# One chunk of three feed-forward stages: seven block products of sums of blocks in place of eight

## The chip, the cores and the metric

The kernel runs on one core of one Trainium2 chip. The metric is the device time of one execution in microseconds. A core has a TensorE (PE; its weight loads are listed apart as PEld), a VectorE (DVE), a ScalarE (ACT), a GpSimd (POOL) and a SyncE (SP), whose queue issues nearly all transfers here. Each engine takes its instructions in order; semaphores tie them together.

## The reference

Two layers of a decoder trunk, for 256 tokens of width 1024, in float32. Each layer is a feed-forward half step, a token mixer, and a second feed-forward half step, each with a norm before and after:

```python
def swiglu(x, w_gate, w_up, w_down):
    return (jax.nn.silu(x @ w_gate) * (x @ w_up)) @ w_down

    for layer in range(DEPTH):
        ng = norm_gains[layer]
        hdn = swiglu(rmsnorm(x, ng[0]), ffn1_w_gate[layer], ffn1_w_up[layer], ffn1_w_down[layer])
        x = x + 0.5 * rmsnorm(hdn, ng[1])
        hdn = rmsnorm(x, ng[2])
        ...
        x = x + rmsnorm(hdn, ng[3])
        hdn = swiglu(rmsnorm(x, ng[4]), ffn2_w_gate[layer], ffn2_w_up[layer], ffn2_w_down[layer])
        x = x + 0.5 * rmsnorm(hdn, ng[5])
```

`w_gate` and `w_up` are 1024 x 2816, `w_down` is 2816 x 1024. The mixers (sparse attention with a state-space branch in layer 0, RWKV-7 in layer 1) are not touched by the change.

## The kernel before

The stages run one after another: f10 (first feed-forward half step of layer 0), the mixer of layer 0, f20, then f11, the mixer of layer 1, f21. The 256 tokens are two tiles of 128, t = 0 and t = 1; the normed input x lies transposed in two tiles, `xth` and `xtl`.

**Numbers.** A float32 product is made of three matmuls: each operand is split into a high and a low part (`hi` rounded, `lo` the rest), and high x high, high x low and low x high are added up in a PSUM bank `acc` (`mm3`). For the weights this split is work on every load: a raw unit of 512 KB lands in `raw`, ScalarE writes `whi` (with the norm's gain `gch`, where there is one), and VectorE writes `wlo` from `raw` and `whi` (`unit`). Both go into a ring of ten pairs of buffers (`rings`: six of the pool ringb, four of ringa). A pair is given back when both token tiles have been multiplied by it.

**A feed-forward stage** (`ffn`) has 66 units in a row: 5 chunks of 512 gate and 512 up columns with 8 units each (one unit is 128 rows k of both), 4 units for the last 256 columns, and 22 units of `w_down`. `lagged` goes through them: unit i is split and multiplied for t = 0, and for t = 1 some units later (`lag`, LAG units at most). After the last row of a chunk, `chunk_end` applies silu and the product with up into `sg`, PE transposes it, and `hth` and `htl` (high and low part) are kept for `w_down`. At the start of a stage, `entry` puts the second token tile's transposes and splits (`prenorm`) between the first units.

**Order.** The program is written in this order; a scheduler in the framework then orders the instructions of each engine inside a stage by its own estimates. Transfers stand in SP's queue in the order of `loads`; one whose buffer is not free holds up those behind it. All instructions of PE, VectorE and ScalarE are issued in `_Engine`'s `call`, so that in the profile of before they stand at L112 (the transfers of the raw units at L288); in the changed file these lines are L130 and L307.

Of the kernel before, what the change touches and what calls it, by code (L numbers as in the profile page):

```python
# [11 lines left out]
F32 = mybir.dt.float32  # L12
F32R = mybir.dt.float32r
# [15 lines left out]
Q_COLS = [(64 * (4 * v + g), 64 * (4 * v + g) + 64) for g in range(4) for v in range(2)]  # L29


def _ffn_units(which, layer):
    units = []
    for c in range(5):
        for k in range(KD):
            units.append((((f"{which}_w_gate", layer), (f"{which}_w_up", layer)), k, 1, [(512 * c, 512 * c + 512)]))
    for h in range(4):
# [22 lines left out]
def _weight_units():  # L60
    a, b, c, o = _mix0_units()
    cg = lambda n: [((n, 0), 4 * h, 4, [(256 * c, 256 * c + 256)]) for c in range(4) for h in range(2)]
    sq = lambda n: [((n, 0), k, 1, [(0, D)]) for k in range(KD)]
    return {
        "f10": _ffn_units("ffn1", 0),
        "m0a": a, "m0x": b, "m0z": c, "m0o": o,
        "f20": _ffn_units("ffn2", 0),
        "f11": _ffn_units("ffn1", 1),
        "m1l": [((("c_w1", 0), ("c_a1", 0)), 0, 8, [(0, 64)])],
        "m1k": cg("c_w_k"),  # L70
        "m1r": cg("c_w_r"),
        "m1g": [(("c_g1", 0), 4 * h, 4, [(0, 160)]) for h in range(2)],
        "m1v": [(("c_w_v", 0), 2 * h, 2, [(512 * c, 512 * c + 512)]) for c in range(2) for h in range(4)],
        "m1o": sq("c_w_o"),
        "f21": _ffn_units("ffn2", 1),
    }


# [19 lines left out]
    return kt, n * sum(hi - lo for lo, hi in cols)  # L98


class _Engine:

    def __init__(self, trunk, engine, kind):
        self.trunk, self.engine, self.kind, self.last = trunk, engine, kind, None

    def __getattr__(self, name):
        f = getattr(self.engine, name)

        def call(out, *a, **k):
            r = f(out, *a, **k)  # L112
            if self.trunk.strict:
# [3 lines left out]
                self.last = r.ins.name  # L117
# [136 lines left out]
class _Trunk:  # L254
# [268 lines left out]
    def lagged(self, units, work, at={}, lag=lambda i: LAG, start=0):  # L523

        pend = []
        for i, u in enumerate(units):
            if i < start:
                continue
            if i in at:
                at[i]()  # L530
            while len(pend) > lag(i - 1):
                work(1, *pend.pop(0))
            w = self.ahead.pop(0) if self.ahead else self.unit(u, self.gain(units, i))
            work(0, i, w)
# [12 lines left out]
    def ffn(self, units, gpost, last, kind, ahead=(), after=None, first=False):  # L547

        nc, tc = self.nc, self.tc
        st = {}  # L550
        hth = {}
        htl = {}

        def chunk_end(t, c, gate, up, n):
            sg = self.wk.tile([P, 512], F32, name="sg", tag="sg", bufs=2)
            r = self.r[t]
            nc.scalar.activation(sg[:, :n], gate, AF.Silu, scale=r)
            nc.vector.scalar_tensor_tensor(sg[:, :n], up, r, sg[:, :n], op0=ALU.mult, op1=ALU.mult)
            if c not in hth:
                hth[c] = hp.tile([P, n // P, S], F32R, name="hth", tag=f"hth{c}")  # L560
                htl[c] = hp.tile([P, n // P, S], F32R, name="htl", tag=f"htl{c}")
# [6 lines left out]
            nc.vector.tensor_sub(htl[c][:, :nj, ts], tp[:, :nj, :], hth[c][:, :nj, ts].bitcast(F32))  # L568

        def work(t, i, w, hs=(0, 1), between=None):  # L570
            wh, wl = w
            ts = slice(P * t, P * t + P)
            xh, xl = [a[:, :, ts] for a in self.xt]
            if i < 40:
                c, k = i // 8, i % 8
# [16 lines left out]
            elif i < 44:  # L592
                c, h = 5, i - 40
                if h == 0:
                    st[t] = self.acc.tile([P, 512], F32, name="acc", tag="acc")
                a = st[t]
                for k in range(2):
                    kk = 2 * h + k
                    self.mm3(a, xh[:, kk, :], xl[:, kk, :], wh[:, k, :], wl[:, k, :], kk == 0, kk == 7)
                if h == 3:  # L600
                    chunk_end(t, c, a[:, :256], a[:, 256:], 256)
            else:
                ft = i - 44
                if ft == 0:
                    for h in hs:
                        st[t, "y", h] = self.acc.tile([P, 512], F32, name="acc", tag="acc")
                for h in hs:
                    self.mm3(st[t, "y", h], hth[ft // 4][:, ft % 4, ts], htl[ft // 4][:, ft % 4, ts],
                             wh[:, 0, 512 * h:512 * h + 512], wl[:, 0, 512 * h:512 * h + 512],
                             ft == 0, ft == 21)  # L610

        n = len(units)
        with tc.tile_pool(name="hp", bufs=1, reuse_waits="tile") as hp, self.work_pool():
            if first:
                self.begin(units, work)
# [1878 lines left out]
    def run(self):  # L2494
# [8 lines left out]
        with self.raw_pool(), ExitStack() as ring:  # L2503
            ring.enter_context(self.ring())
            self.ffn(ph["f10"], 1, 2, "mixer", ph["m0a"], first=True)
            self.mix0(ph, 3, 2, ring, self.y1)
            self.ffn(ph["f20"], 5, 6, "ffn", ph["f11"])
            a, b = [self.ringa], self.rings[:1]
            self.rings = a * 4 + (b * 6 + a * 2) * 2 + (b * 6 + a * 4) * 4 + b * 6
            self.count = len(self.ahead)  # L2510
            self.ffn(ph["f11"], 7, 8, "plain", after=lambda: self.mix1_start(ph["m1l"][0]))
        y = self.mix1(ph, 9, self.y1)
        with self.raw_pool(side="right"), self.ring():
            with self.work_pool():
                row = self.row(9, tag="raw", bufs=None, pool=self.raw)
                self.prepare(ph["f21"], 1)
                self.postnorm(1, y, row, False)
            self.ffn(ph["f21"], 11, None, "out")
        banks.close()


# [85 lines left out]
```

## Time and profile before

| | before |
|---|---|
| median of 3 runs | 1171.52 us (1171.45 to 1172.55) |
| profiled execution | 1170.79 us |
| its span | 1169.0 us, mean granted clock 0.999 |
| PE busy | 1153.5 us, 6855 matmuls |
| VectorE busy | 778.9 us |
| ScalarE busy | 598.1 us |
| moved | 192.43 MB, 165 GB/s on average |

The span goes from the first to the last instruction in the profile; the time of an execution holds a little more around it. Busy times are those of the profiled execution. PE is listed as busy for nearly the whole span; how near it is to its own limit is read from the spacing of its matmuls and from what it waits for. The page's sums are means over six unlike stages; the change touches three of them, f20 (about 383 to 569 us in the span), f11 (569 to 756) and f21 (980 to 1165).

### The profile page before, as it was taken

How to read it: one execution, taken by the hardware profiler on the slowest of the kernel's cores; microseconds unless marked ns; L12 is line 12 of the kernel's file. 1: busy time of each engine (PE TensorE's matmuls, PEld its weight loads, DVE VectorE, ACT ScalarE, POOL GpSimd, SP SyncE). 2: the span in 40 equal slices, each digit the busy share in tenths (PEclk: the TensorE clock that was granted, in tenths of full speed). 3: DMA queues.
4: the chain of work that ended last, by engine and by line, in shares of the span. 5: the costliest groups of instructions: out<-in, count | busy, mean ns of one | idle time of the engine just before them, and what ended most of it. 6: DMA issues, size and time to landing. Idle time of an engine off the chain costs nothing.

```text
span 1169.0 us, 17703 instructions
## 1 busy us (share of the span) xinstructions
PE 1153.5 (99%) x6855; PEld 975.2 (83%) x6855; DVE 778.9 (67%) x1310; ACT 598.1 (51%) x1000; POOL 17.3 (1%) x46
## 2 busy tenths in 40 slices
PE   9999999999999999999999999999999999999997
PEld 7888888898998788888888888899988887888886
DVE  6675547888779855554856555578885797655543
ACT  6655445677575655543555544375054145645431
POOL 0000000000000000000000000002100000000000
PEclk9999999999999999999999999999999999999999
DMA  8866564443335765555456555711334123765540
GB/s 288 282 209 187 180 201 145 148 136 102 108 128 166 241 207 186 189 181 184 149 190 225 189 180 198 261 37 57 112 110 146 36 95 121 241 207 185 180 162 37
DMA packets 54163, 192.43 MB, mean 165 GB/s; under 512 B 6653, under 2 KB 6653, under 8 KB 53950
## 3 DMA queue, kind: packets, MB, share of 16 engines
q1 hardware_dynamic: 54078, 191.30, 49.9%
q8 instruction: 54, 0.88, 0.3%
q14 instruction: 31, 0.25, 0.1%
HBM read 190.22 MB, written 1.05 MB: 164 GB/s over the span
## 4 chain that ended last, share of the span: by engine, by line
PE 92%; DVE 4%; DMA 1%; ACT 1%; issue 1%; SPq 0%; DVEq 0%; ACTq 0%; POOL 0%; POOLq 0%
PE acc L112 87%; PE tp L112 5%; DMA raw<-in_wst_dram 1%; DVE wlo L112 1%; ACT whi L112 1%; ACT junk L112 0%; DVE rs_a L112 0%; DVE xu L112 0%; DVE tm L112 0%; DVE lc L112 0%; DVE x L112 0%; DVE rs_y L112 0%; SPq L288 0%; DVE wl L112 0%; ACT aT L112 0%
## 5 line engine op out<-in xcount | busy, mean ns | idle before, releaser
L112 DVE SCALAR_TENSOR_TENSOR wlo<-raw,gch,whi 128x1024 fp32r<-128x1024 f32 (+2 forms) x211 | 236.3, 1133 | 125.8 <-ACT whi L112 125.4
L112 ACT ACTIVATE whi<-raw,gch 128x1024 fp32r<-128x1024 f32 (+2 forms) x211 | 213.2, 1029 | 151.3 <-PE acc L112 99.4
L112 PE MATMUL acc<-whi,xth 128*128 128x512 f32 (+1 forms) x576 | 224.4, 393 | 0.8 <-ACT whi L112 0.6
L112 PE MATMUL acc<-wlo,xth 128*128 128x512 f32 (+1 forms) x576 | 223.2, 389 | 0.2 <-DVE wlo L112 0.2
L112 PE MATMUL acc<-whi,xtl 128*128 128x512 f32 (+1 forms) x576 | 222.8, 388 | 0.0
L112 DVE TENSOR_TENSOR wlo<-raw,whi 128x1024 fp32r<-128x1024 f32 x112 | 137.1, 1224 | 116.2 <-ACT whi L112 115.9
L112 ACT CAST whi<-raw 128x1024 fp32r<-128x1024 f32 x112 | 117.7, 1051 | 124.7 <-PE acc L112 110.4
L112 PE MATMUL acc<-whi,hth 128*128 128x512 f32 x352 | 137.5, 391 | 0.0
L112 PE MATMUL acc<-whi,htl 128*128 128x512 f32 x352 | 137.0, 389 | 0.0
L112 PE MATMUL acc<-wlo,hth 128*128 128x512 f32 x352 | 137.0, 389 | 0.0
L112 PEld LDWEIGHTS acc<-whi,xth 128*128 128x128 f32 x576 | 108.1, 188 | 23.0 <-ACT whi L112 1.5
L112 PEld LDWEIGHTS acc<-whi,xtl 128*128 128x128 f32 x576 | 108.1, 188 | 21.9 <-DVE xtl L112 0.4
L112 PEld LDWEIGHTS acc<-wlo,xth 128*128 128x128 f32 x576 | 108.2, 188 | 21.2 <-DVE wlo L112 0.6
L112 PE MATMUL acc<-whi,xt 128*128 128x512 f32 x352 | 111.0, 391 | 0.0
L112 PEld LDWEIGHTS acc<-whi,htl 128*128 128x128 f32 x352 | 66.1, 188 | 13.8
L112 PEld LDWEIGHTS acc<-whi,hth 128*128 128x128 f32 x352 | 66.1, 188 | 13.6
L112 PEld LDWEIGHTS acc<-wlo,hth 128*128 128x128 f32 x352 | 66.1, 188 | 13.5
L112 PEld LDWEIGHTS acc<-whi,xt 128*128 128x128 f32 x352 | 66.0, 188 | 13.5
L112 PE MATMUL acc<-wlo,xt 128*128 128x512 f32 x176 | 69.0, 392 | 0.0
L112 PE MATMUL acc<-xnh,whi 128*128 128x256 f32 x160 | 46.6, 291 | 0.0
L112 PE MATMUL acc<-xnl,whi 128*128 128x256 f32 x160 | 45.2, 282 | 0.0
L112 PE MATMUL acc<-xnh,wlo 128*128 128x256 f32 x160 | 45.2, 282 | 0.0
(369 smaller groups left out, 1673.7 us busy)
## 6 DMA issues: line engine op xcount, KB each, us to landing
raw<-in_wst_dram SPq DMA_DIRECT2D x300, 512.0 KB, 3.6
lw<-in_wst_dram SPq DMA_DIRECT2D x12, 512.0 KB, 3.5
grow<-in_rows_dram SPq DMA_DIRECT2D x8, 512.0 KB, 4.8
wlo<-in_wst_dram SPq DMA_DIRECT2D x8, 512.0 KB, 3.7
whi<-in_wst_dram SPq DMA_DIRECT2D x8, 512.0 KB, 4.2
wr<-in_wst_dram SPq DMA_DIRECT2D x8, 512.0 KB, 5.7
rows<-in_rows_dram SPq DMA_DIRECT2D x3, 512.0 KB, 5.4
lw<-in_lw_dram SPq DMA_DIRECT2D x3, 512.0 KB, 3.6
```

Source lines behind the costliest of these rows:

```text
L112: r = f(out, *a, **k)
```

## The change

In f20, f11 and f21 (not in f10), chunk 3 (`WIDE`) of the gate and up columns is computed as a product of 2 x 2 blocks: rows are the two token tiles, the inner dimension is halved (4 of the 8 rows k each), columns are gate and up. The eight block products of the plain way become seven, of sums and differences of blocks.

- *Loads.* Chunk 3's eight units become four of 1 MB, issued after the units k = 4 to 7 of chunk 2. Two land in a new buffer `wa`, two in a buffer `hx`, and ScalarE scales them in place with the gain.
- *Sums of x* (`sums`, at unit 10): VectorE adds `xth` and `xtl` to x again, forms four sums of blocks, and splits them with ScalarE into `sumh` and `suml`. `pin` ties the first of these instructions to stand behind VectorE's last instruction written so far.
- *Products* (`spread(None)`, before chunk 4): seven phases of two ring units with six matmuls each, 84 matmuls where there were 96. Before a phase VectorE forms, where needed, the difference or sum of two weight blocks in place; then ScalarE casts and VectorE subtracts, as for any weight. Three partial results are copied by ScalarE to `u` tiles, and VectorE adds a bank to each.
- *Both token tiles* take part in every phase, so the lag of t = 1 goes down towards chunk 3 and up again behind it. `rings`' order changes with it.
- `hth` and `htl` of chunks 3 to 5 are kept in `hx`, which is first the room for the sums, then for raw weights. In f20 and f21 the row of gains for the norm behind the stage is fetched into an `xp` tile before the last four loads, and a small VectorE copy goes away.

```diff
+WIDE = 3
-def _ffn_units(which, layer):
+def _ffn_units(which, layer, wide=False):
     for c in range(5):
+        if wide and c == WIDE:
+            continue
         for k in range(KD):
             units.append((..., k, 1, [(512 * c, 512 * c + 512)]))
+            if wide and c == WIDE - 1 and k > 3:
+                j = k - 4
+                units.append((..., 2 * j, 2, [(512 * WIDE, 512 * WIDE + 512)]))
...
     def lagged(self, units, work, at={}, lag=lambda i: LAG, start=0, wide=None):
+            if _ffn_part(u)[0] == "w":
+                wide(u)
+                continue
+            if wide and _ffn_part(u) == ("g", WIDE + 1, 0):
+                while pend:
+                    work(1, *pend.pop(0))
+                wide(None)
...
+        def spread(unit):
+            if unit is not None:
...
+                if j % 2 == 0:
+                    raws[j] = wa[:, j // 2]
+                else:
+                    if j == 1:
+                        st["raw"] = space(F32)
+                    raws[j] = st["raw"][:, j // 2, 0:8]...
+                self.loads.append(self.fetch(raws[j], src, after=self.loads[-1]))
+                for i in range(2):
+                    nc.scalar.activation(raws[j][:, i], raws[j][:, i], AF.Copy, scale=g[:, i])
+                return
...
+            def phase(bank, a, b, start, before=lambda p: None):
+                for p in range(2):
+                    before(p)
+                    ring = self.rings[self.count % len(self.rings)]
+                    self.count += 1
+                    hi, lo = [ring.tile([P, 2, 512], F32R, name=g, tag=g) for g in ("whi", "wlo")]
+                    x = b(p)
+                    nc.scalar.copy(hi, x)
+                    nc.vector.tensor_sub(lo, x, hi.bitcast(F32))
+                    for j in range(2):
+                        k = 2 * p + j
+                        nc.tensor.matmul(bank, a[0][:, k], hi[:, j], ...)
+                        nc.tensor.matmul(bank, a[0][:, k], lo[:, j], ...)
+                        nc.tensor.matmul(bank, a[1][:, k], hi[:, j], ...)
+            q, r, z = acc(), acc(), acc()
+            phase(q, half(row0, 0), lambda p: g0[p], True)
+            m1 = temp()
+            nc.scalar.copy(m1, q)
+            phase(r, form(0), lambda p: t1, True, lambda p: sub(t1, u0[p], g0[p]))
+            m5 = temp()
+            nc.scalar.copy(m5, r)
+            def inner(p):
+                sub(u0[p], u1[p], u0[p])
+                nc.vector.tensor_add(g0[p], u0[p], g0[p])
+            phase(q, form(1), lambda p: g0[p], False, inner)
+            u2 = temp()
+            nc.scalar.copy(u2, q)
+            phase(r, form(3), lambda p: u1[p], False)
+            nc.vector.tensor_add(u2, u2, r)
+            phase(q, form(2), lambda p: u0[p], False)
+            nc.vector.tensor_add(m5, m5, q)
+            phase(z, half(row0, 1), lambda p: g1[p], True)
+            nc.vector.tensor_add(m1, m1, z)
+            phase(q, half(row1, 1), lambda p: g1[p], False, lambda p: sub(g1[p], g1[p], g0[p]))
+            chunk_end(0, WIDE, m1, u2, 512, m1)
+            chunk_end(1, WIDE, q, m5, 512)
+
+        def sums():
+            hi, lo = [self.xp.tile([P, 4, 4, P], F32R, name=n, tag="x8") for n in ("sumh", "suml")]
+            w = space(F32)
...
+            nc.vector.pin = True
+            for h in range(2):
+                a = [v[:, 4 * h:4 * h + 4].bitcast(F32) for v in self.xt]
+                nc.vector.tensor_add(x[:, 4 * h:4 * h + 4], *a)
+            nc.vector.tensor_add(f[:, 0], a21, a22)
+            nc.vector.tensor_sub(f[:, 1], f[:, 0], a11)
+            nc.vector.tensor_sub(f[:, 2], a11, a21)
+            nc.vector.tensor_sub(f[:, 3], a12, f[:, 1])
+            for h in range(2):
+                nc.scalar.copy(hi[:, hs], f[:, hs])
+                nc.vector.tensor_sub(lo[:, hs], f[:, hs], hi[:, hs].bitcast(F32))
...
+        def lag(i):
+            return min(LAG - 2 * (i == LAG - 1) - (LAG <= i < n - 8), max(0, (24 - i) // 2) if i < 28 else max(1, (i - 30) // 4))
...
+            space = lambda dt: hp.tile([P, 2, 10, S], dt, name="hx", tag="hx")
+            if wide:
+                wa = hp.tile([P, 2, 2, D], F32, name="wa")
...
-                rows = [self.row(gpost, after=hth[1].bitcast(F32)[:, 0, 0:1]), None]
+                row = self.xp.tile([P, 2, D], F32, name="rows", tag="x8")[:, 0]
+                self.fetch(row, self.rows[gpost].partition_broadcast(P), self.loads[-4])
+                rows = [row, None]
```

The instructions of f10 and of both mixers stand in the same order as before; what moves lies in the three stages. The first place is VectorE at the start of f20, behind the splits of the second token tile (`xtl`); the rows `rs_...` belong to the norm's square root. Before:

```order
L112 TENSOR_TENSOR xtl<-tp,xth 128x4x128
L112 TENSOR_SCALAR rs_h<-rs_h 128x1
L112 SCALAR_TENSOR_TENSOR rs_y<-rs_a,rs_y 128x1
L112 TENSOR_SCALAR rs_y<-rs_h 128x1
L112 SCALAR_TENSOR_TENSOR wlo<-raw,gch,whi 128x1024
```

And after the change:

```order
L130 TENSOR_TENSOR xtl<-tp,xth 128x4x128
L130 TENSOR_SCALAR rs_h<-rs_h 128x1
L130 SCALAR_TENSOR_TENSOR rs_y<-rs_a,rs_y 128x1
L130 TENSOR_TENSOR hx<-xth,xtl 128x1024
L130 TENSOR_SCALAR rs_y<-rs_h 128x1
L130 SCALAR_TENSOR_TENSOR wlo<-raw,gch,whi 128x1024 x2
```

The first addition of the sums stands now ahead of the split of the stage's sixth unit.

The second place is VectorE around chunk 3 of f20. Before, it holds gained splits of the weights, with `sg` and `htl` of the chunks between:

```order
L112 SCALAR_TENSOR_TENSOR wlo<-raw,gch,whi 128x1024
L112 SCALAR_TENSOR_TENSOR sg<-acc,rs_y,sg 128x512
L112 SCALAR_TENSOR_TENSOR wlo<-raw,gch,whi 128x1024 x2
L112 TENSOR_TENSOR htl<-tp,hth 128x4x128
L112 SCALAR_TENSOR_TENSOR wlo<-raw,gch,whi 128x1024 x2
```

After, the same stretch (`wa` and `hx` as a source of `wlo` are weights of chunk 3 or combinations of them):

```order
L130 TENSOR_TENSOR htl<-tp,hth 128x4x128
L130 TENSOR_TENSOR wlo<-wa,whi 128x1024
L130 SCALAR_TENSOR_TENSOR sg<-acc,rs_y,sg 128x512
L130 TENSOR_TENSOR wa<-wa 128x2x512
L130 TENSOR_TENSOR wlo<-hx,whi 128x1024 x2
L130 TENSOR_TENSOR hx<-hx 128x2x512 x2
L130 TENSOR_TENSOR htl<-tp,hth 128x4x128
L130 TENSOR_TENSOR hx<-hx 128x2x512
L130 TENSOR_TENSOR wlo<-hx,whi 128x1024
L130 TENSOR_TENSOR wlo<-wa,whi 128x1024
```

Combinations and plain splits have taken the place of the gained splits, and there are more of them in a row.

The third place is PE in chunk 3 of f20 after the change (acc_4443 and acc_4444 are the banks q and r of `spread`; acc_4629, acc_4630 and acc_4649 belong to chunk 4):

```order
L130 MATMUL acc_4444<-whi_4528,suml_4082 128x512
L130 MATMUL acc_4629<-whi_4625,xth_3821 128x512
L130 MATMUL acc_4630<-whi_4625,xth_3821 128x512
L130 MATMUL acc_4649<-whi_4625,xth_3821 128x512
L130 MATMUL acc_4443<-whi_4539,sumh_4081 128x512
L130 MATMUL acc_4443<-wlo_4540,sumh_4081 128x512
L130 MATMUL acc_4443<-whi_4539,suml_4082 128x512
```

Before, chunks 3 and 4 alternated between the token tiles:

```order
L112 MATMUL acc_4393<-whi_4473,xth_3826 128x512
L112 MATMUL acc_4393<-wlo_4474,xth_3826 128x512
L112 MATMUL acc_4393<-whi_4473,xtl_3827 128x512
L112 MATMUL acc_4394<-whi_4473,xth_3826 128x512
L112 MATMUL acc_4394<-wlo_4474,xth_3826 128x512
```

A phase of chunk 3 takes one bank for both halves of the inner dimension, and the scheduler has put the first matmuls of chunk 4 between two phases.

On SP's queue the four pieces of 1 MB stand between the last raw units of chunk 2:

```order
L307 DMA raw<-in_wst_dram 128x1024 x16
L307 DMA wa<-in_wst_dram 128x2048
L307 DMA raw<-in_wst_dram 128x1024
L307 DMA hx<-in_wst_dram 128x2048
L307 DMA raw<-in_wst_dram 128x1024
```

Before, 22 raw units of 512 KB stood there in a row, and 102 more behind the next gain row.

More of the change, by code (lines that the diff above doesn't have):

```diff
@@ L66, in _weight_units @@
         "m0a": a, "m0x": b, "m0z": c, "m0o": o,
-        "f20": _ffn_units("ffn2", 0),
-        "f11": _ffn_units("ffn1", 1),
+        "f20": _ffn_units("ffn2", 0, True),
+        "f11": _ffn_units("ffn1", 1, True),
         "m1l": [((("c_w1", 0), ("c_a1", 0)), 0, 8, [(0, 64)])],
@@ L74, in _weight_units @@
         "m1o": sq("c_w_o"),
-        "f21": _ffn_units("ffn2", 1),
+        "f21": _ffn_units("ffn2", 1, True),
     }
@@ L98, in _unit_cols, with _ffn_part @@
     return kt, n * sum(hi - lo for lo, hi in cols)
+def _ffn_part(unit):
+    src, k0, kt, cols = unit
+    if not isinstance(src[0], tuple):
+        return "d", 0, k0
+    if kt == 1:
+        return "g", cols[0][0] // 512, k0
+    return ("w", WIDE, k0 // 2) if cols[0][1] - cols[0][0] == 512 else ("h", 5, k0 // 2)
 class _Engine:
     def __init__(self, trunk, engine, kind):
-        self.trunk, self.engine, self.kind, self.last = trunk, engine, kind, None
+        self.trunk, self.engine, self.kind, self.last, self.pin = trunk, engine, kind, None, False
     def __getattr__(self, name):
@@ L116, in call @@
                     self.trunk.tc.add_manual_dep(r.ins, self.last, info, reason="order")
-                self.last = r.ins.name
+            self.last = r.ins.name
             if self.trunk.plan is not None:
@@ L521, in prepare, with lagged @@
             self.ahead.append(self.unit(units[i], self.gain(units, i)))
-    def lagged(self, units, work, at={}, lag=lambda i: LAG, start=0):
+    def lagged(self, units, work, at={}, lag=lambda i: LAG, start=0, wide=None):
         pend = []
@@ L545, in entry, with ffn @@
         return {LAG - 1: lambda: self.prenorm(1), LAG + 2: turn}
-    def ffn(self, units, gpost, last, kind, ahead=(), after=None, first=False):
+    def ffn(self, units, gpost, last, kind, ahead=(), after=None, first=False, wide=None):
         nc, tc = self.nc, self.tc
@@ L552, in ffn, with chunk_end @@
         htl = {}
-        def chunk_end(t, c, gate, up, n):
-            sg = self.wk.tile([P, 512], F32, name="sg", tag="sg", bufs=2)
+        def chunk_end(t, c, gate, up, n, sg=None):
+            if sg is None:
+                sg = self.wk.tile([P, 512], F32, name="sg", tag="sg", bufs=2)
             r = self.r[t]
@@ L559, in chunk_end @@
             if c not in hth:
-                hth[c] = hp.tile([P, n // P, S], F32R, name="hth", tag=f"hth{c}")
-                htl[c] = hp.tile([P, n // P, S], F32R, name="htl", tag=f"htl{c}")
+                if c < WIDE:
+                    hth[c], htl[c] = [hp.tile([P, n // P, S], F32R, name=g, tag=f"{g}{c}") for g in ("hth", "htl")]
+                else:
+                    if c == WIDE:
+                        st["hx"] = space(F32R)
+                    hx = st["hx"]
+                    hth[c], htl[c] = [hx[:, i, 4 * (c - WIDE):4 * (c - WIDE) + n // P] for i in range(2)]
             nj = n // P
@@ L568, in chunk_end @@
             nc.vector.tensor_sub(htl[c][:, :nj, ts], tp[:, :nj, :], hth[c][:, :nj, ts].bitcast(F32))
+        raws = {}
+        def spread(unit):
+            if unit is not None:
+                j = _ffn_part(unit)[2]
+                kt, n = _unit_cols(unit)
+                src = self.wst[self.offset:self.offset + P * kt * n].rearrange("(p k n) -> p k n", p=P, k=kt)
+                self.offset += P * kt * n
+                if j % 2 == 0:
+                    raws[j] = wa[:, j // 2]
+                else:
+                    if j == 1:
+                        st["raw"] = space(F32)
+                    raws[j] = st["raw"][:, j // 2, 0:8].rearrange("p a b -> p (a b)").rearrange("p (k n) -> p k n", k=2)
+                self.loads.append(self.fetch(raws[j], src, after=self.loads[-1]))
+                g = self.gain([unit], 0)
+                for i in range(2):
+                    nc.scalar.activation(raws[j][:, i], raws[j][:, i], AF.Copy, scale=g[:, i])
+                return
+            g0, u0, g1, u1 = [[raws[2 * i + p][:, :, 512 * m:512 * m + 512] for p in range(2)] for i in range(2) for m in range(2)]
+            t1 = st["raw"][:, :, 8:10].rearrange("p i a b -> p i (a b)")
+            acc = lambda: self.acc.tile([P, 512], F32, name="acc", tag="acc")
+            temp = lambda: self.wk.tile([P, 512], F32, name="u", tag="w2k", bufs=3)
+            xh, xl = self.xt
+            row0, row1 = [[a[:, :, P * t:P * t + P] for a in (xh, xl)] for t in range(NT)]
+            half = lambda x, h: [a[:, 4 * h:4 * h + 4] for a in x]
+            sub = lambda out, a, b: nc.vector.tensor_sub(out, a, b)
+            def phase(bank, a, b, start, before=lambda p: None):
[9 more added lines that the diff above has]
+                        k = 2 * p + j
+                        first, last = start and k == 0, k == 3
+                        nc.tensor.matmul(bank, a[0][:, k], hi[:, j], start=first, stop=False, skip_group_check=not start)
+                        nc.tensor.matmul(bank, a[0][:, k], lo[:, j], start=False, stop=False, skip_group_check=not start)
+                        nc.tensor.matmul(bank, a[1][:, k], hi[:, j], start=False, stop=last, skip_group_check=not start)
+            form = lambda i: [a[:, i] for a in st["sums"]]
+            q, r, z = acc(), acc(), acc()
[20 more added lines that the diff above has]
+            chunk_end(1, WIDE, q, m5, 512)
@@ L602, in work @@
             else:
-                ft = i - 44
+                ft = k
                 if ft == 0:
@@ L2506, in run @@
             self.mix0(ph, 3, 2, ring, self.y1)
-            self.ffn(ph["f20"], 5, 6, "ffn", ph["f11"])
             a, b = [self.ringa], self.rings[:1]
-            self.rings = a * 4 + (b * 6 + a * 2) * 2 + (b * 6 + a * 4) * 4 + b * 6
+            self.rings = (b * 6 + a * 4) * 5 + (b * 6 + a * 2) * 2 + b * 6 + a * 4 + b
+            self.ffn(ph["f20"], 5, 6, "ffn", ph["f11"], wide=True)
+            self.rings = a * 4 + (b * 6 + a * 4) * 2 + (b * 6 + a * 2) * 4 + (b * 6 + a * 4) + b * 6
             self.count = len(self.ahead)
-            self.ffn(ph["f11"], 7, 8, "plain", after=lambda: self.mix1_start(ph["m1l"][0]))
+            self.ffn(ph["f11"], 7, 8, "plain", after=lambda: self.mix1_start(ph["m1l"][0]), wide=True)
         y = self.mix1(ph, 9, self.y1)
@@ L2517, in run @@
                 self.postnorm(1, y, row, False)
-            self.ffn(ph["f21"], 11, None, "out")
+            self.ffn(ph["f21"], 11, None, "out", wide=True)
         banks.close()
```

21 lines of the change are left out of this document (14 added, 7 removed).

## The prediction

> **What bounds the kernel now.** I read the page's sums first, then the chain that ended last.
>
> ```profile
> span 1169.0 us, 17703 instructions
> PE 1153.5 (99%) x6855; PEld 975.2 (83%) x6855; DVE 778.9 (67%) x1310; ACT 598.1 (51%) x1000; POOL 17.3 (1%) x46
> PE 92%; DVE 4%; DMA 1%; ACT 1%; issue 1%; SPq 0%; DVEq 0%; ACTq 0%; POOL 0%; POOLq 0%
> ```
>
> PE is on 92% of the chain, VectorE on 4%. A busy PE need not be a PE at its peak, so I looked in the chain, in order of time (start, length, what, count), at its longest pieces in f20 and in f11.
>
> ```profile
> 514.30 47.64 PE acc L112 x210
> ...
> 700.90 48.99 PE acc L112 x216
> ```
>
> 47.64 / 210 = 0.2269 and 48.99 / 216 = 0.2268 us from one matmul of 512 columns to the next, with nothing between them. That is the price of a matmul here. Next, what PE waits for over the whole span (total us, times, longest):
>
> ```profile
> PE tp L112 <- DVE identr L112: 1.6, 1, 1.6
> PE tp L112 <- DVE x L112: 1.4, 2, 0.8
> ...
> PE acc L112 <- DVE wlo L112: 0.2, 1, 0.2
> ```
>
> Missing weights cost PE 0.2 us in all. The three stages that change, by windows (f20, f11, f21), and two stretches for the DMA rate:
>
> ```profile
> core 0: us, PE busy (x) PEld busy (x) DVE busy (x) ACT busy (x) POOL busy (x), PEclk, DMA share, GB/s
> 383.00:569.00 186.00, 185.76 (x846) 153.55 (x845) 111.11 (x141) 95.03 (x114) 0.00 (x0) 1.00 0.59 192
> 569.00:756.00 187.00, 186.66 (x873) 155.12 (x871) 107.38 (x138) 91.34 (x117) 2.17 (x9) 1.00 0.62 208
> 980.00:1165.00 185.00, 180.94 (x822) 149.17 (x820) 103.16 (x126) 87.15 (x104) 0.00 (x0) 1.00 0.52 171
> 575.00:665.00 90.00, 90.00 (x412) 74.49 (x411) 55.31 (x53) 48.25 (x53) 0.00 (x0) 1.00 0.65 211
> 0.00:29.00 29.00, 26.57 (x113) 20.71 (x114) 17.75 (x26) 18.80 (x25) 0.92 (x7) 1.00 0.86 288
> ```
>
> In f20 PE is busy for 185.76 of 186 us at a granted clock of 1.00, VectorE for 111, ScalarE for 95. The 75 us in which VectorE idles there are explained by the waits of f20:
>
> ```profile
> DVE wlo L112 <- ACT whi L112: 65.7, 57, 2.9
> ACT whi L112 <- PE acc L112: 57.4, 36, 3.0
> ```
>
> VectorE waits for ScalarE, and ScalarE for PE to give a pair of the ring back. Both run ahead of PE until the ring is full; their idle time is surplus, and that is what the change spends.
>
> **The change, part by part.** *Removed.* Chunk 3 of a changed stage had 8 rows x 2 token tiles x 2 halves x 3 = 96 matmuls of 512 columns; seven phases of 12 make 84. Three stages save 36 matmuls: 36 x 0.2268 = 8.16 us on the engine that bounds. Transposes stay as they are. The new matmuls take one operand from the ring and one from the sums, 128x128 against 128x512, as those before do.
>
> *Added on VectorE and ScalarE.* Durations of the nearest forms in f20 (busy, mean ns; idle before):
>
> ```profile
> L112 DVE SCALAR_TENSOR_TENSOR wlo<-raw,gch,whi 128x1024 fp32r<-128x1024 f32 x41 | 52.5, 1284 | 33.4 <-ACT whi L112 33.3
> L112 ACT ACTIVATE whi<-raw,gch 128x1024 fp32r<-128x1024 f32 x40 | 45.6, 1152 | 36.3 <-PE acc L112 28.4 <-DMA raw<-in_wst_dram 4.5 <-issue 3.1
> ...
> L112 PEld LDWEIGHTS acc<-wlo,xth 128*128 128x128 f32 x176 | 33.1, 188 | 7.1 <-DVE wlo L112 0.6
> ...
> L112 DVE TENSOR_TENSOR wlo<-raw,whi 128x1024 fp32r<-128x1024 f32 x22 | 26.9, 1225 | 28.8 <-ACT whi L112 28.8
> L112 ACT CAST whi<-raw 128x1024 fp32r<-128x1024 f32 x22 | 23.2, 1053 | 30.4 <-PE acc L112 26.1 <-issue 4.1
> ...
> L112 DVE SCALAR_TENSOR_TENSOR sg<-acc,rs_y,sg 128x512 f32<-128x512 f32 x10 | 7.5, 748 | 2.2 <-ACT sg L112 2.0
> L112 DVE TENSOR_TENSOR htl<-tp,hth 128x512 fp32r<-128x512 f32 x10 | 6.9, 688 | 3.8 <-ACT hth L112 3.8
> ...
> L112 ACT CAST hth<-tp 128x512 fp32r<-128x512 f32 x10 | 5.8, 575 | 6.4 <-PE tp L112 6.4
> ...
> L112 DVE TENSOR_TENSOR u<-acc,grow 128x512 f32<-128x512 f32 x4 | 2.7, 683 | 0.1
> ```
>
> VectorE per stage: minus 8 gained splits (8 x 1.284 = 10.3), plus 14 plain splits (14 x 1.225 = 17.2), 8 combinations of weight blocks (8 x 1.225 = 9.8), 3 adds with a PSUM bank (3 x 0.683 = 2.0), and the sums: 2 adds and 2 splits of 128x1024 and 4 adds of 128x512 (4 x 1.225 + 4 x 0.688 = 7.7). Net +26.4 us. ScalarE: minus 8 x 1.152, plus 8 scalings in place at the same price, 14 casts (14.7), 2 casts of sums (2.1), 3 copies of a bank (1.7): +18.5 us. VectorE has 75 us of surplus in f20 and ScalarE 91, so as an average both fit. Combinations in place (128x2x512, f32) and adds that read a bank have no row of their own; lower bound the 0.683 of a 128x512 form for an add and 1.225 for a combination, upper bound the 1.284 of the three-operand form for either. I take the lower ends, which are the rows of the same operation and size.
>
> *Is the cover there where it is needed?* I laid VectorE's new order of f20 out with these durations, against PE's new order at 0.2268 us a matmul. Between the matmul that ends the use of the first ring pair that a phase takes, and the matmul that reads the last split of the last phase, PE has 47.3 us of work (208 matmuls: chunk 3's, what is left of chunk 2, and chunk 4's first, which the new order puts between phases). In that stretch VectorE has 14 plain splits, 7 combinations, 4 gained splits of chunk 4, 4 `sg` and 5 `htl`: 17.2 + 8.6 + 5.1 + 3.0 + 3.4 = 37.3 us. It is 10 us short of PE's work, and the smallest margin at any one matmul came to 3.4 us in f20, 3.8 in f11, 3.8 in f21 (all at chunk 4's first unit or chunk 2's last transposes). So PE waits for none of it: cost 0, hidden behind these matmuls. If the cover were gone, see rival B.
>
> *Loads.* The stage loads the same bytes, in four pieces of 1 MB after the raws of chunk 2's rows 4 to 7. The SP queue is in order: behind a 1 MB piece whose buffer is not free stand the raws of chunk 2, and ScalarE behind them. The pieces' buffers are new ones, or free since the sums (the `hx` space), at the time they are issued. From the first 1 MB piece to chunk 3's first phase PE has 37 us, for 6.3 MB (four pieces of 1.05 MB, four raws of 0.52): 170 GB/s. The windows show 211 GB/s over 90 us of f11, where the ring sets the pace, and 288 in the first 29 us. Cost 0, with 7 us in hand at 211 GB/s. The gain row of f20 and f21 moves to before the last four loads and needs no VectorE copy now: 512 KB that move, no time.
>
> *Exposed.* At unit 10 the sums are pinned behind the second token tile's split. The first add (1.22 us) thus goes ahead of a weight split that PE soon reads. The three places, in order of time (start, us):
>
> ```profile
> 385.55 1.29 DVE L112 SCALAR_TENSOR_TENSOR wlo<-raw,gch,whi 128x1024 fp32r<-128x1024 f32 x1
> ...
> 388.12 0.39 PE L112 MATMUL acc<-wlo,xth 128*128 128x512 f32 x1
> ...
> 571.42 0.69 DVE L112 TENSOR_TENSOR xtl<-tp,xth 128x512 fp32r<-128x512 f32 x1
> ...
> 572.27 1.28 DVE L112 SCALAR_TENSOR_TENSOR wlo<-raw,gch,whi 128x1024 fp32r<-128x1024 f32 x1
> ...
> 574.68 0.39 PE L112 MATMUL acc<-wlo,xth 128*128 128x512 f32 x1
> ...
> 984.31 1.28 DVE L112 SCALAR_TENSOR_TENSOR wlo<-raw,gch,whi 128x1024 fp32r<-128x1024 f32 x1
> ...
> 986.35 0.39 PE L112 MATMUL acc<-wlo,xt 128*128 128x512 f32 x1
> ```
>
> f20: the split ends at 386.84, PE reads it at 388.12: margin 1.28 against 1.22, so 0 to 0.1 us. f11: xtl ends at 572.11, then add and split end at about 574.6, against 574.68: 0. f21: the add starts soon after the split of xt, at about 984.0, add and split end at 986.55, against 986.35: 0.2. Sum 0.3 us; bounds 0 (margins a little larger) and 3 x 1.22 = 3.7 (nothing hidden). I take 0.3, by the margins of the very places.
>
> **Sum.** 8.16 - 0.3 = 7.9 us. The profiled execution took 1170.79 us (span 1169.0 and 1.79 around it) and becomes 1162.9. The median of the runs shown, 1171.52, lies 0.73 above: 1163.6.
>
> [...] The rows above say 0.2268 us in two pieces of over 200 matmuls. [...]
>
> **The rivals.**
> *A, the forecast*: all added work hidden, 1163.6; its own range 1162.9 to 1165.
> *B, the cover falls short*: it would if splits of chunk 3 could start only as chunk 3 itself begins (no ring pair or no raw free earlier). Then VectorE has 14 x 1.225 + 6 x 1.225 + 3 x 0.748 + 3 x 0.688 = 28.8 us to do while PE has 26.1 (115 matmuls, with those of chunk 4 between): 2.7 us lost per stage, 8.1 in all, which eats the gain: about 1171.5. For it speaks that VectorE has little in hand even with the longer stretch (37.3 of 47.3 us), against it the 57.4 us in which ScalarE waited for free ring pairs in f20 alone, and that the new ring tables and lags hand them out ahead.
> *C, slower*: the forms without a row are dearer. Margin 3.4 us a stage; the gain of a stage is 2.72, and 0.78 more (a third of 2.34) makes it slower by over 0.2%: 6.9 us a stage of late work. Over the 10 combinations and adds ahead of the last split this is 0.69 us each, a combination of 1.9 us instead of 1.225. The rows speak against it: 1225 and 1284 ns for two and three operands of 1024 columns. Or the 1 MB pieces come late, and ScalarE, in order, stands before one: at 156 GB/s 6.3 MB take 40.4 us, 3.4 over the 37, which three times is 10.2; from there down it decides. Either way 1174 and more.
> *D, a removed matmul is worth less than its spacing*: PE's time in f20 might be held by its weight loads, 0.188 us each by the row above, and the removed ones be worth only that: 36 x 0.188 = 6.8, less 0.3: 1165.0. Against it stand the pieces of the chain. [...]
>
> **How the numbers follow.** A measurement of this kernel can tell about 0.2%, 2.34 us, from no change: faster is under 1169.2, slower over 1173.9. Chances: A 0.84, D 0.04, B 0.07, C 0.05. A and D are faster (0.88), B is the same (0.07), C slower (0.05). Range: below, the full 8.16 us from 1171.45 gives 1163.3, and runs of one kernel differ by 1.1 us here, so 1162.0. Above, it goes over D's 1165.0 and towards B to 1168.0, with the exposed adds at their upper bound (8.16 - 3.7 = 4.5, 1167.0) inside. B and C lie outside with 0.12.
>
> **What the profile of the changed kernel would show.** PE with 36 fewer matmuls, x6819, and about 1145 us busy; VectorE 779 + 3 x 26.4 = 858, ScalarE 598 + 55 = 654; the bytes as before. Windows of f20, f11 and f21 each about 2.6 us shorter, the other stages the same. In PE's waits at most some tenths for `wlo` at the start of f21; the chain 91 to 92% PE. I am wrong if PE's waits name a split from `wa` or `hx`, or an add `u`, with microseconds in chunk 3 (B or C by combinations: a `hx<-hx` group well over 1.3 us), if ScalarE waits for a DMA into `wa` or `hx` (C by loads), or if PE's pieces have a spacing other than 0.227.

## The result, and the profile after

The changed kernel takes 1163.97 us (median of 4 runs, 1163.72 to 1164.29) against 1171.49 us before (now a median of 4 runs); the ratio is 0.9935, with a 95% interval of 0.9923 to 0.9947. 1163.6 was forecast. The page after, the lines that answer to those of before:

```profile
span 1162.1 us, 17699 instructions
PE 1145.4 (99%) x6819; PEld 968.4 (83%) x6819; DVE 843.7 (73%) x1383; ACT 644.2 (55%) x1057; POOL 17.2 (1%) x46
PE 90%; DVE 5%; DMA 2%; ACT 1%; issue 1%; SPq 0%; DVEq 0%; POOL 0%; ACTq 0%; POOLq 0%
```

PE has 36 matmuls and 8.1 us less, VectorE and ScalarE have 65 and 46 us more, and PE still makes up nearly all of the chain. What PE waits for over the span:

```profile
PE tp L130 <- DVE identr L130: 1.6, 1, 1.6
...
PE tp L130 <- DVE sg L130: 1.1, 1, 1.1
PE acc L130 <- ACT whi L130: 0.8, 1, 0.8
...
PE acc L130 <- DVE wlo L130: 0.2, 1, 0.2
```

No wait for a `u`, and none for a split of `wa` or `hx`: the list is that of before but for some tenths. Where the time came from is read from PE's timeline, from one landmark to the next: the first transposes of f10, of f20, the mixer of layer 1, the first transposes of f21. First before, then after:

```profile
36.03 0.63 PE L112 MATMUL tp<-ident,sg 128*128 128x128 f32 x4 [0.39 <-DVE sg L112]
382.12 1.29 PE L112 MATMUL tp<-ident,x 128*128 128x128 f32 x8 [0.82 <-DVE x L112]
751.10 0.46 PE L112 MATMUL acc<-hT,lws 128*128 128x128 f32 x2 [0.34 <-POOL lb L1668]
980.89 0.63 PE L112 MATMUL tp<-ident,x 128*128 128x128 f32 x4 [0.59 <-DVE x L112]
```
```profile
36.75 0.52 PE L130 MATMUL tp<-ident,sg 128*128 128x128 f32 x3 [1.10 <-DVE sg L130]
382.83 1.29 PE L130 MATMUL tp<-ident,x 128*128 128x128 f32 x8 [0.81 <-DVE x L130]
746.39 0.46 PE L130 MATMUL acc<-hT,lws 128*128 128x128 f32 x2 [0.33 <-POOL hsel L1787]
976.19 1.07 PE L130 MATMUL tp<-ident,x 128*128 128x128 f32 x6 [0.60 <-DVE x L130]
```

| stretch | before | after | difference |
|---|---|---|---|
| start to f10's first `sg` | 36.03 | 36.75 | +0.72 |
| rest of f10, mixer 0 | 346.09 | 346.08 | 0 |
| f20 and f11 | 368.98 | 363.56 | -5.42 |
| mixer 1 | 229.79 | 229.80 | 0 |
| f21 to the end | 188.1 | 185.9 | -2.2 |

f20 and f11 give 24 matmuls at 0.226 us, all that was expected; f11's first transposes (at 569.48 us before, 567.45 after) part them into 2.7 us each. f21 gives 2.2 of 2.7. The 0.72 us at the start of f10 lies in instructions that the change leaves alone: ScalarE stood 0.92 us before a raw unit, where it stood 0.23 before. In the profiles below whose f10 is the same, the first transposes of `sg` start anywhere from 36.00 to 37.12 us; so I take it for scatter of the loads at the start.

Now the stages by windows (f20, f11, f21 of the changed kernel), the stretch of VectorE's dense work around chunk 3 of f20, and the 28 us ahead of it:

```profile
core 0: us, PE busy (x) PEld busy (x) DVE busy (x) ACT busy (x) POOL busy (x), PEclk, DMA share, GB/s
381.90:567.30 185.40, 184.31 (x841) 152.33 (x841) 135.04 (x170) 111.44 (x137) 0.00 (x0) 1.00 0.56 193
567.30:751.40 184.10, 183.76 (x861) 152.66 (x859) 128.44 (x161) 106.12 (x134) 2.09 (x9) 1.00 0.58 204
974.60:1157.10 182.50, 179.17 (x813) 147.33 (x811) 124.68 (x154) 103.01 (x123) 0.00 (x0) 1.00 0.50 174
428.00:464.00 36.00, 36.00 (x167) 29.84 (x166) 35.72 (x36) 28.02 (x33) 0.00 (x0) 1.00 0.23 77
400.00:428.00 28.00, 28.00 (x131) 23.20 (x130) 21.11 (x22) 22.81 (x25) 0.00 (x0) 1.00 0.89 338
```

Over a stage VectorE still idles for 50 to 58 us, but in the fourth row for 0.28 us of 36. PE is busy throughout that stretch, because the splits come a few us before they are read. The tightest reads of split weights in f20 and in f11, ScalarE's writing of `whi` and the matmul that takes it:

```profile
456.49 1.16 ACT L130 ACTIVATE whi<-raw,gch 128x1024 fp32r<-128x1024 f32 x1
...
460.77 0.61 PE L130 MATMUL acc<-whi,xth 128*128 128x512 f32 x2
```
```profile
634.54 1.05 ACT L130 CAST whi<-wa 128x1024 fp32r<-128x1024 f32 x1
...
639.24 0.61 PE L130 MATMUL acc<-whi,xth 128*128 128x512 f32 x2
```

460.77 - 457.65 = 3.1 us in hand in f20, 639.24 - 635.59 = 3.65 in f11; the smallest of f21 is 2.9 (a `whi` of chunk 4's first unit, as in f20; that of f11 belongs to chunk 3). The transposes of `sg` are tighter still. In f21, chunk 2:

```profile
1041.81 1.40 DVE L130 SCALAR_TENSOR_TENSOR sg<-acc,rs_y,sg 128x512 f32<-128x512 f32 x2
...
1044.91 1.03 PE L130 MATMUL tp<-ident,sg 128*128 128x128 f32 x8
```

The two `sg` are done at 1042.55 and 1043.21, the four transposes of each start at 1044.91 and 1045.34: 2.1 us in hand at the second. Matched in this way, the four `sg` of chunks 1 and 2 have 1.8 to 3.5 us in hand in f20, 2.4 to 3.2 in f11 and 1.9 to 2.4 in f21; before the change they had 3.9 to 4.4. So the change did eat into the cover, without using it up.

### The profile page after: what moved, and what is told of

The parts are those of the page before. It is cut to its first block, busy times and chain, and to the rows that moved or that the text cites. A ratio compares the mean times of both kernels' runs of the same rounds, so it can differ in the third digit from the quotient of the medians.

```text
span 1162.1 us, 17699 instructions
## 1 busy us (share of the span) xinstructions
PE 1145.4 (99%) x6819; PEld 968.4 (83%) x6819; DVE 843.7 (73%) x1383; ACT 644.2 (55%) x1057; POOL 17.2 (1%) x46
## 4 chain that ended last, share of the span: by engine, by line
PE 90%; DVE 5%; DMA 2%; ACT 1%; issue 1%; SPq 0%; DVEq 0%; POOL 0%; ACTq 0%; POOLq 0%
PE acc L130 86%; PE tp L130 4%; DMA raw<-in_wst_dram 2%; DVE wlo L130 1%; ACT whi L130 1%; ACT junk L130 0%; DVE rs_a L130 0%; DVE Gx L130 0%; DVE xu L130 0%; DVE tm L130 0%; DVE lc L130 0%; DVE x L130 0%; SPq L307 0%; DVE rs_y L130 0%; DVE wl L130 0%
## 5 line engine op out<-in xcount | busy, mean ns | idle before, releaser
L130 DVE SCALAR_TENSOR_TENSOR wlo<-raw,gch,whi 128x1024 fp32r<-128x1024 f32 (+2 forms) x187 | 204.2, 1112 | 48.5 <-ACT whi L130 48.3
L130 ACT ACTIVATE whi<-raw,gch 128x1024 fp32r<-128x1024 f32 (+2 forms) x187 | 184.7, 1012 | 85.7 <-DMA raw<-in_wst_dram 42.1
L130 PE MATMUL acc<-whi,xth 128*128 128x512 f32 (+1 forms) x536 | 206.5, 392 | 1.0 <-ACT whi L130 0.8
L130 PE MATMUL acc<-whi,xtl 128*128 128x512 f32 (+1 forms) x536 | 206.6, 389 | 0.0
L130 PE MATMUL acc<-whi,hx 128*128 128x512 f32 x320 | 102.3, 390 | 0.0
L130 PE MATMUL acc<-whi,hth 128*128 128x512 f32 x192 | 75.1, 391 | 0.0
L130 PE MATMUL acc<-whi,htl 128*128 128x512 f32 x192 | 74.8, 389 | 0.0
L130 PE MATMUL acc<-wlo,hth 128*128 128x512 f32 x192 | 74.7, 389 | 0.0
L130 PEld LDWEIGHTS acc<-whi,hx 128*128 128x128 f32 x320 | 60.1, 188 | 12.5
L130 PE MATMUL acc<-wlo,hx 128*128 128x512 f32 x160 | 62.3, 389 | 0.0
```

## The experiments

Theory A: the gain is 36 matmuls at their spacing on PE, and all that was added is hidden, save a few tenths at the stages' starts. L, S and U are three views of how much cover VectorE's work has: up to the smallest margin at a single read (L), up to the idle time of the whole stage (S), or none (U). Each edited program is ordered anew by the scheduler, so in the edited stages instructions change their places besides what the edit says.

**What a matmul is worth** (e_mm2). Every matmul of the phases twice.

```diff
-                        nc.tensor.matmul(bank, a[0][:, k], hi[:, j], start=first, stop=False, ...)
+                        for m in range(2):
+                            nc.tensor.matmul(bank, a[0][:, k], hi[:, j], start=first and m == 0, stop=False, ...)
...
```

> The changed kernel with each matmul of the seven phases issued twice (chunk 3's block products come out doubled): 84 more matmuls of 512 columns in each of three stages, 252 in all, and nothing more on VectorE or ScalarE. Theory A (a matmul in this stream is worth its spacing, 0.2268 us): 252 x 0.2268 = 57.2 us, from 1164.0 to about 1221. Rival D (worth only its weight load, 0.188 us): 47.4 us, 1211. [...]

Measured: 1221.15 us, 57.2 more than the changed kernel, so 0.227 us for each of 252 matmuls. The chain in f20's chunk 3 (start, length, what, count):

```profile
452.68 35.41 PE acc L130 x156
```

35.41 / 156 = 0.227. Rival D is refuted: its 0.188 us does not hold in this stream.

**One stage alone** (e_f21). f20 and f11 as before.

```diff
-        "f20": _ffn_units("ffn2", 0, True),
-        "f11": _ffn_units("ffn1", 1, True),
+        "f20": _ffn_units("ffn2", 0),
+        "f11": _ffn_units("ffn1", 1),
...
```

> The change in f21 alone; f20 and f11 with the units, lags and ring order of before. Theory A: 12 matmuls x 0.2268 = 2.72 us less, of which 0.3 go back at the stage's start: 2.4 us faster than before, 1169.1, ratio 0.9979. If the gain came from something else that the change brings to all three stages at once (the rows of gains, the ring's order in f20 and f11), less: 1170 to 1171.5.

Measured: 1169.24 us, ratio 0.9982 (0.9973 to 0.9992), 2.0 us faster than the 1171.27 of before beside it. That is near the 2.2 us of f21 in the profiles above; with the 2.7 us each of f20 and f11 there, the gain goes by the stage. f20 and f11 were not run alone.

**Less VectorE work** (e_nocomb).

```diff
-            sub = lambda out, a, b: nc.vector.tensor_sub(out, a, b)
+            sub = lambda out, a, b: None
...
```

> The changed kernel without the eight combinations of weight blocks in each of the three stages (the phases multiply the plain blocks, so chunk 3 comes out as something else); splits, sums, bank adds and matmuls stay. 8 x 1.22 = 9.8 us less VectorE work a stage. Theory A and L (what VectorE does there lies beside matmuls, and the tightest split has 3 us in hand): no change, 1163.5 to 1164.3. Rival (VectorE's work in chunk 3 is part of what bounds): up to 29 us faster; already 1 us would speak for it.

Measured: 1164.30 us (1163.71 to 1164.90), the same. VectorE's page row falls from 843.7 to 818.2 us:

```profile
PE 1145.9 (99%) x6819; PEld 969.1 (83%) x6819; DVE 818.2 (70%) x1359; ACT 644.6 (55%) x1057; POOL 17.2 (1%) x46
```

Taking work away from a stretch in which VectorE never rests gained nothing here: it was early enough already.

**More VectorE work, in four doses** (e_dve2, e_dve4, e_dve7, e_dve14). The split of a ring unit is written again, in 2, 4, 7 phases' first units, or in all 14 units.

```diff
                     nc.vector.tensor_sub(lo, x, hi.bitcast(F32))
+                    if p == 0:
+                        nc.vector.tensor_sub(lo, x, hi.bitcast(F32))
```

> The changed kernel with the split of the first ring unit of each phase written twice by VectorE: 7 x 1.22 = 8.5 us more VectorE work in chunk 3 of each of three stages, nothing else. Theory L (VectorE runs without a pause there, and what counts are the 3 to 4 us by which the tightest split is early): six of the seven repeats, 7.3 us, stand ahead of the tightest split, so 7.3 less 3 to 4 = 3.4 to 4.4 us are lost in a stage, somewhat less in f11, where VectorE pauses for some us: 8 to 13 us in all, 1172 to 1177. Theory S (the stage's surplus of VectorE counts, some 45 us of idle time a stage): nothing lost, 1164. Theory U (VectorE's added work is never hidden): 25.6 us, 1190.

> The changed kernel with the split of every ring unit of the seven phases written twice: 14 x 1.22 = 17.1 us more VectorE work in chunk 3 of each of three stages. Theory L: twelve repeats, 14.6 us, stand ahead of the tightest split, so some 10 to 12 us are lost a stage, 28 to 36 in all, 1192 to 1200. Theory S: nothing lost, 1164. Theory U: 51 us, 1215.

> As the run with seven repeats, but the split is written twice only in the first two phases: 2 x 1.22 = 2.4 us more VectorE work in chunk 3 of each stage, less than the 2.9 to 3.7 us by which the tightest read of a stage was early. Theory L (hidden up to the smallest margin, lost beyond it): nothing lost, 1164.0 to 1164.5. Theory U (each us costs a us): 1171.3. A loss that goes with the added work from the first us on, at the 20.9 / 25.6 of the seven repeats: 1170.

> The split written twice in the first four phases: 4.9 us more a stage. Theory L: 4.9 less the margins of 3.1, 3.7 and 2.9 us: 1.8 lost in f20, 1.2 or less in f11 (VectorE pauses there), 2.0 in f21, 4 to 5 in all, 1168 to 1169, with the TensorE clock at full rate. If already waits of about 2 us bring the halved clock that the run with seven repeats showed for 6.8 us at a time (3.4 us lost each): 3.4 to 10 more, 1171 to 1179. Theory U: 14.7 us, 1178.7.

| repeats in a stage | more VectorE work in all, us | measured, us | over the changed kernel |
|---|---|---|---|
| 2 | 7.3 | 1163.68 | -0.3 |
| 4 | 14.6 | 1172.80 (1169.42 to 1174.76) | +8.8 |
| 7 | 25.6 | 1184.90 (1183.05 to 1186.74) | +20.9 |
| 14 | 51.2 | 1202.15 | +38.2 |

Two repeats cost nothing, so U and every loss in proportion fall; the reserve is nearly used up there, though: in f20 the first of chunk 2's last two `sg` is done at 450.82 us and its transposes start at 451.42. S falls with four. Up to the smallest margin the work is free, beyond it not: that is L. But from four repeats on more is lost than L had worked out. With four repeats PE's two large waits (from f20 on) are

```profile
PE acc L130 <- DVE wlo L130: 3.4, 2, 3.2
PE acc L130 <- ACT whi L130: 2.1, 1, 2.1
```

5.5 us, somewhat over the 4 to 5 expected, and shared out otherwise: 3.2 us in f20 (1.8 expected), none in f11 (up to 1.2), 2.1 in f21 (2.0). In f20 PE waits for a `wlo` of chunk 4's first unit, which in the changed kernel was ready 5.1 us before its read (459.05, 464.17): with the repeats in it the stage is ordered anew, and the tightest read is another one. The rest is the clock, in the windows ahead of the wait, in it, and behind it:

```profile
455.00:462.00 7.00, 7.00 (x37) 5.88 (x35) 7.00 (x8) 5.21 (x7) 0.00 (x0) 1.00 0.01 2
462.00:469.00 7.00, 3.79 (x16) 2.84 (x15) 7.00 (x8) 3.80 (x4) 0.00 (x0) 0.93 0.45 150
469.00:472.00 3.00, 3.00 (x10) 2.35 (x9) 3.00 (x4) 2.25 (x3) 0.00 (x0) 0.60 0.77 244
472.00:475.00 3.00, 3.00 (x15) 2.47 (x14) 2.91 (x3) 1.44 (x2) 0.00 (x0) 1.00 0.77 255
```

The wait of 3.2 us ends at 468.3; the granted clock falls to half at 468.0, for 3.41 us, and matmuls come 0.427 us apart. A second stretch of 3.41 us follows the wait of 2.1 us in f21. Each costs at most 1.7 us, half its length: 5.5 and at most 3.4 make 8.9 of the 9.9 us by which this profile's span is longer, the rest being f10's start (0.4) and tenths. The ten executions part in the same way: three took 1169.4 to 1170.2 us at a mean granted clock of 0.997 or 0.998, seven took 1172.3 to 1174.8 at 0.995. The shortest is 5.5 us over the changed kernel, as much as the waits alone. With seven repeats PE's waits are

```profile
PE acc L130 <- ACT whi L130: 5.2, 2, 3.7
PE acc L130 <- DVE wlo L130: 3.4, 4, 2.2
PE acc L130 <- DVE u L130: 2.7, 1, 2.7
...
PE acc L130 <- ACT u L130: 0.7, 1, 0.7
```

12.0 us, within the 8 to 13 of theory L, and two stretches of 6.83 us at half clock, in parts of which PE waits, cost at most 6.8 more: at most 18.8 of 19.1. With fourteen repeats the clock is at half for 20.5 us in all. So with four and seven repeats L has the sum of the waits about right; it lacked the clock, and the places where the waits fall.

Half clock followed a wait of 2.1 us in f21 of e_dve4, then. Yet not every such wait is followed by it. In f11 of e_dve14 (the wait and, behind it, a window at clock 1.00):

```profile
674.25 1.20 PE L130 MATMUL acc<-whi,xth 128*128 128x512 f32 x4 [2.11 <-ACT whi L130]
...
676.00:682.00 6.00, 5.92 (x26) 4.92 (x27) 6.00 (x7) 1.94 (x3) 0.00 (x0) 1.00 0.49 164
```

What tells the two apart, no run shows.

**The start of a stage** (e_nopin, e_pin2). First without the pin, then with both additions pinned.

```diff
-            nc.vector.pin = True
             for h in range(2):
+                nc.vector.pin = True
                 a = [v[:, 4 * h:4 * h + 4].bitcast(F32) for v in self.xt]
```

> The changed kernel without the pin: both additions of xth and xtl go ahead of the split of the stage's sixth unit, where one does now. Theory A (the exposed step: the add's 1.21 us against the margin that the split had before, 1.28, 1.12 and 0.75 us): two adds take 2.43 us, so PE waits 1.15 us in f20, 1.3 in f11, 1.7 in f21, 4.1 in all where the changed kernel has some 0.4: 1167.7. Rival (adds there are hidden as the rest is): 1164.0.

> The changed kernel with both additions pinned, so that none goes ahead of the sixth unit's split. Theory A: the waits at the start of f11 (0.1 us) and f21 (0.3) go away: 1163.6, not to be told from 1164.0 by the time alone; in the trace the spacings at the start of f21 come down from 0.439 and 0.341 to 0.227 us, and f21 is 0.3 us shorter. Rival (these waits come from elsewhere, for instance from the cast of the sums on ScalarE): they stay.

Without the pin: 1165.81 us (0.9953, 0.9938 to 0.9968), 1.8 more; f20 and f11 together 1.5 us longer, f21 0.6. The direction is A's, the size half of its 3.7, and the waits are not the ones that A named. In f20 and in f11 PE waits for ScalarE:

```profile
389.38 0.73 PE L130 MATMUL acc<-whi,xth 128*128 128x512 f32 x2 [0.44 <-ACT whi L130]
...
574.09 0.73 PE L130 MATMUL acc<-whi,xth 128*128 128x512 f32 x2 [0.57 <-ACT whi L130]
```

In this program's new order these matmuls of a later unit stand ahead of the reads of the late split; only in f21 does PE wait for a `wlo` behind the adds, twice. So the run shows that two adds there cost more than one, not that they cost it in the way A has it. With both pinned: 1163.73 us, not to be told apart, but the trace shows the step. f21's start in the changed kernel:

```profile
979.31 1.22 DVE L130 TENSOR_TENSOR hx<-xt 128x1024 f32<-128x1024 f32 x1
980.44 0.16 DVE L130 SCALAR_TENSOR_TENSOR rs_a<-rs_a 128x1 f32<-128x1 f32 x1
980.51 2.48 DVE L130 SCALAR_TENSOR_TENSOR wlo<-raw,gch,whi 128x1024 fp32r<-128x1024 f32 x2
...
981.18 0.61 PE L130 MATMUL acc<-whi,xt 128*128 128x512 f32 x2
981.85 0.50 PE L130 MATMUL acc<-wlo,xt 128*128 128x512 f32 x1
```

and with both pinned:

```profile
979.79 1.28 DVE L130 SCALAR_TENSOR_TENSOR wlo<-raw,gch,whi 128x1024 fp32r<-128x1024 f32 x1
...
981.13 0.39 PE L130 MATMUL acc<-wlo,xt 128*128 128x512 f32 x1
```

In the first, the add runs ahead of the split, the split is ready at 981.79, and the matmul that reads it starts 0.44 us after the one before it (at 981.41). In the second no add is there, the split ends at 981.07, and f21's matmuls as a whole take 0.4 us less (177.5 against 177.9 from the start of the first transposes to that of the last matmul). So the add ahead of the split is the one that has no pin, the second half's.

**The fourth stage** (e_best, e_best15, e_tab36). f10 done the same way, with both additions pinned: first as it stands, then with the sums later, then also with the mixer's tables and constants loaded later and the pieces of work on its compression weights (`compress_bias`) moved back with them. The diff shows the last of the three.

```diff
-        "f10": _ffn_units("ffn1", 0),
+        "f10": _ffn_units("ffn1", 0, True),
...
-                at = {4: ..., 5: ..., 16: self.tables, 20: self.constants, **dict(zip(range(24, 44, 2), self.compress_bias()))}
+                at = {4: ..., 5: ..., 15: sums, 36: self.tables, 37: self.constants, **dict(zip(range(38, 58, 2), self.compress_bias()))}
```

> The changed kernel with both additions pinned and chunk 3 of f10 done the same way too (its first load goes to the buffer of the 1 MB pieces, since the other has no room for it). Theory A: 12 matmuls more are saved, 2.72 us, and 0.4 at the stage starts: 1160.9, ratio to before 0.9910. Theory L as a rival: in f10 VectorE has less in hand at the same place, since the weights of the mixer's compression (some 10 instructions of VectorE) stand there too; where the tightest split is late by over 0.9 us nothing is left of the 2.7.

Measured: 1163.44 us (1161.96 to 1164.12), ratio 0.9930 (0.9917 to 0.9942): at most half a us better than the changed kernel. PE loses time in f10:

```profile
44.02 0.50 PE L130 MATMUL acc<-whi,xth 128*128 128x512 f32 x1 [1.95 <-ACT sg L130]
```

The norm's square roots stood behind the sums on VectorE, the silu waited for them, and PE for the bank that the silu frees. ScalarE was no earlier: behind late raw units and the casts of the sums it came free at 43.19 us, and the square root was done at 43.24. This profile is the shortest of the five executions, at a mean granted clock of 0.998; the three of 1163.4 us and more list 0.996 or 0.997, and no trace shows where in them the clock was lower.

> All four stages with the seven products, both additions pinned, and in f10 the sums at unit 15 in place of 10, behind the norm's square roots, whose delay held up the first chunk's silu (PE waited 1.95 us for it in the run before). Theory A: the 1.95 us go, 1161.5 to 1162 by the faster of the executions before, at best 1160.9. Rival (f10 is held by its loads there, and the wait only comes elsewhere): 1163 to 1164.

Measured: 1163.03 us, ratio 0.9931 (0.9918 to 0.9943). The wait went, and another came, down a chain of three (waits from 20 to 60 us):

```profile
ACT wa L130 <- DMA wa<-in_wst_dram: 4.6, 1, 4.6
...
DVE hx L130 <- ACT wa L130: 3.2, 1, 3.2
...
PE tp L130 <- DVE sg L130: 2.2, 1, 2.2
```

This is the prediction's rival C by loads, in the stage that the change had left out: ScalarE, in order, stands before a 1 MB piece. A stretch of 3.41 us at half clock follows the 2.2 us.

> As the run before with four stages, and the mixer's tables and constants (0.75 MB, then 1 MB) loaded in f10 behind chunk 4 in place of in chunk 2. In the run before, ScalarE stood 4.6 us before the first 1 MB piece of f10, VectorE 3.2 us behind it, and PE 2.2 us for a silu behind that. Theory A with late loads as the cause (rival C of the prediction, in f10): 0.75 MB less ahead of the piece is some 3 us at 250 GB/s, so the wait goes, and f10 gives its 2.7 us: 1160.5 to 1161.2. Rival (f10's start is short of bandwidth as a whole, and the next piece or raw unit is late instead): 1162.5 to 1163.5.

Measured: 1161.23 us (1160.70 to 1162.84), ratio 0.9915 (0.9902 to 0.9929), 2.7 us under the changed kernel; its highest run, 1162.84, is under the lowest of that kernel, 1163.72. Its median is 1.8 us under that of e_best15, but the two intervals overlap. The same waits are shorter, and PE's for `sg` is 1.1 us, with no half clock behind it:

```profile
ACT wa L130 <- DMA wa<-in_wst_dram: 2.6, 2, 2.2
...
DVE hx L130 <- ACT wa L130: 1.6, 1, 1.6
```

The later loads and the later work on the compression weights were not tried apart, nor were the later loads with the old f10.

## Why the prediction was right, step by step

- *36 matmuls at 0.2268 us*: right, by the stretches of f20 and f11 (24 for 5.42 us) and by e_mm2.
- *26.4 us more on VectorE, 18.5 on ScalarE, per stage*: right as sums of durations. All VectorE durations of the trace add up to 825.5 us before and 903.9 after, 26.1 a stage; ScalarE's to 653.0 and 708.2, 18.4 a stage. For VectorE the page shows 21.6, and 843.7 where I had 858, since it counts a time once in which two instructions overlap: in f21's rows above, the add of 1.22 us is followed after 1.13. The unseen forms took the lower ends that I had chosen:

```profile
L130 DVE TENSOR_TENSOR wlo<-hx,whi 128x1024 fp32r<-128x1024 f32 x8 | 9.7, 1219 | 0.1
...
L130 DVE TENSOR_TENSOR hx<-hx 128x1024 f32<-128x1024 f32 x4 | 4.9, 1221 | 0.1
...
L130 DVE TENSOR_TENSOR u<-u,acc 128x512 f32<-128x512 f32 x3 | 2.0, 680 | 0.0
```

- *The cover*: right in what it was for: PE waits for none of the work in chunk 3. The margins were taken too large: 3.4, 3.8 and 3.8 us worked out; 3.1, 2.9 and 2.1 measured at the places named (chunk 4's first unit in f20, chunk 2's last transposes in f11 and f21), and less at the transposes of chunk 1, which I had not named (1.8 us in f20). The 10 us between VectorE's 37.3 and PE's 47.3 us were no reserve: VectorE runs without a pause there, and five us more a stage already make PE wait.
- *The loads*: right, PE did not wait for them. They were faster than I had assumed (338 GB/s from 400 to 428 us, ahead of chunk 3 in f20; 229 in the same window before).
- *The exposed adds*: 0.3 us forecast. f20 0, f11 0.1, f21 0.33 measured, as spacings beyond 0.227 us. The reason was told wrongly: it is not the pinned addition that goes ahead of the split, but the other one.
- *Rival B, and C by dearer forms*: refuted. Rival C's price for late work was too low, as e_dve4 shows: waits of 2.1 and 3.2 us were followed there by half clock as well, at up to 1.7 us for each stretch of 3.41.
- *Missing from the sum*: 0.7 us of f10's start in the profiled execution, and 0.3 us between the issue of the last output transfer and the end, which I can't explain: it is 3.8 us where it was 3.5 before, and short again with f10 changed too. That the median came within 0.4 us of the forecast is in part luck: f10's start alone scatters by 1.1 us from profile to profile.

## What to carry to other kernels

Where one engine bounds and the others wait for it through a full ring, fewer instructions on the bounding engine were worth their spacing here (0.227 us a matmul), and more work on the others was free up to the smallest margin at a single read (two repeats, 7.3 us in all, cost nothing; four, 14.6 us, cost 8.8), not up to the idle time of the stage. Lay the new order out with measured durations and look for that read. Then compare the next stage's conditions before repeating the trick there: in f10 the same change gave next to nothing (at most half a us) until loads and other work ahead of it were moved (2.7 us).

## What the runs showed of the hardware that was not expected

After some waits of PE in the middle of a dense stream (3.2 and 2.1 us in e_dve4, 2.2 in e_best15) the granted clock fell to half for 3.41 us, with matmuls 0.427 us apart in e_dve4; after others it did not (2.11 us in e_dve14, 1.95 in the profile of e_best). So of waits of about 2 us, two cost nothing more and two up to 1.7 us more. What tells them apart is not shown; no run was made to test it.

Around the issue of the four pieces of 1 MB (410.5 to 415.3 us) one core's loads reached 338 GB/s over 28 us (400 to 428 us), where the kernel before moved 229 GB/s in the same window.
